# RWKV-7 chunk inverse on two chunks at a time, and norms per head spread by one product with ones

## The chip, the core and the metric

One NeuronCore of a Trainium2 chip runs the whole program. Its engines each work through their own instructions in order: TensorE (PE, with weight loads shown as PEld), VectorE (DVE), ScalarE (ACT), GpSimd (POOL), and SyncE (SP), which issues the DMAs. The metric is the device time of one execution in microseconds, the median of several runs.

## The reference

Two layers on 512 tokens of width 1024, in fp32. Each layer is half a SwiGLU feed-forward (1024 to 2816 and back), a mixer, and another half feed-forward, all with RMS norms. The mixer of layer 0 is RWKV-7 on 8 heads of 64 beside a block attention (MoBA) on 8 heads of 64. The mixer of layer 1 is HGRN2, a gated linear attention with 8 heads of 128. What the change touches:

```python
kk = _heads(k * k_k, RWKV_HEADS).astype(f32)
kk = kk * lax.rsqrt(jnp.maximum(jnp.sum(kk * kk, axis=-1, keepdims=True), 1e-24))
...
def step(state, inp):
    r_t, w_t, k_t, v_t, kk_t, a_t = inp
    sa = jnp.einsum('bhvk,bhk->bhv', state, -kk_t)
    state = (state * w_t[:, :, None, :]
             + jnp.einsum('bhv,bhk->bhvk', sa, kk_t * a_t)
             + jnp.einsum('bhv,bhk->bhvk', v_t, k_t))
    return state, jnp.einsum('bhvk,bhk->bhv', state, r_t)
...
y = ((y - mean) * lax.rsqrt(var + LNX_EPS)).reshape(bsz, seq, RWKV_DIM) * lnx_w + lnx_b
...
o = o * lax.rsqrt(jnp.mean(o * o, axis=-1, keepdims=True) + EPS)   # HGRN2, per head
```

## The kernel before

The tokens are split in two streams A and B of 256. Activations lie with the channel on the partitions. A long list of jobs, written out by hand in `build`, is the backbone: a job is one weight tile of 128 x 1024 (some 128 x 768), used in 24 (18) products of 256 columns into a PSUM bank `m`. Each weight is split in two planes for precision: `split_hi` copies the raw tile `wr` to `wh` on ScalarE, `split_lo` writes the rest to `wl` on VectorE, and `mm3` issues the three products hi x hi, hi x lo, lo x hi. Both planes have three buffers (`AHEAD + 1`). At the start of job n the program emits the split of job n + 2, behind the evictions of the job that has just ended.

Everything else runs as tasks: Python generators that emit a few instructions and yield. After every `mm3` a planner, `fill`, steps at most as many tasks as its own clock allows; the clock (`Clock`, `Eng`) keeps an assumed free time of each engine. These lines decide it:

```python
full = max(free["dve"], free["act"]) > now + self.left + BACK
for t in self.eligible():
    if t.ready <= max(now, free[t.eng]) + LEAD and (t.first or not full):
        self.step(t)
```

`left` is what remains of the current job by the planner's clock and `BACK` is 1 us. `need` forces a task to its end before the jobs behind it; it stands before the second stream's `proj0` blocks (`tail1`) and before the output projections.

The tasks that the change touches, per block q of 128 tokens (four in all), two chunks c of 64 tokens in each:

- `rw_front`: low-rank gates; the squares of k (`kk`); sums per head by four products with `sel` (two columns each) into a bank of 128 x 8; `rsqrt` on 128 x 8 (two integer operations, three Newton steps of three operations each); `bcast`, eight products of the broadcast result with the identity, which put the value of a head on all its partitions; then `kk` is scaled from PSUM.
- `rw_prep`, per chunk: the matrices `AR`, `BK`, `Ga`, `Gr`, then the start of the inverse (`X`, `Xt`).
- `rw_inv`, per chunk: five levels of a block inverse, each in two steps: eight products Ga x X into `zb`, a ScalarE copy to `Z`; eight products Z x Xt into `wt` and (but for the last level) eight Xt x Z into `wb`, written under a mask into `Xt` and `X` by VectorE.
- `rw_chain`, per chunk in order: the state.
- `rw_tail`: mean and variance per head; the same sums, `rsqrt` and `bcast` as in `rw_front`; gate; split to the planes of `y`.
- `hg_out` (HGRN2): output and state per four heads; sums of squares by eight products with `ones` (one column each); `rsqrt` on 128 x 8; for each four heads, four broadcast products with the identity, then scale, gate and split.

In the profile every instruction has the line of the wrapper in `Eng`, L176, so groups are told apart by their tiles: `b` is any of the five small PSUM banks of the tasks, `kms`, `rqi`, `rqy`, `rqz` are the tiles of the narrow `rsqrt`, and `cst` holds `ident`, `sel`, `blk` and `ones`. An fp32 product is two MATMUL instructions in the trace.

Of the kernel before, what the change touches and what calls it, by code (L numbers as in the profile page):

```python
# [26 lines left out]
EPS = 1e-6  # L27
# [163 lines left out]
class K:  # L191
# [85 lines left out]

    def rmask(self, i):
        return self.msk[:, i * 64:i * 64 + 64].unsqueeze(1).to_broadcast([128, 4, 64])

# [171 lines left out]
    def rsqrt(self, x, w, tag="rqy"):  # L452
        v = self.v
        i = self.t(self.hp, [128, w], I32, "rqi", 4)
        y = self.t(self.hp, [128, w], F32, tag, 4)
        z = self.t(self.hp, [128, w], F32, "rqz", 4)
        v.tensor_single_scalar(i, x.bitcast(I32), 1, op=ALU.logical_shift_right)
        v.tensor_scalar(y.bitcast(I32), i, -1.0, float(0x5f3759df), op0=ALU.mult, op1=ALU.add)
        for _ in range(3):
            v.tensor_tensor(z, x, y, op=ALU.mult)  # L460
            v.scalar_tensor_tensor(z, z, -0.5, y, op0=ALU.mult, op1=ALU.mult)
            v.scalar_tensor_tensor(y, z, 1.5, y, op0=ALU.add, op1=ALU.mult)
        return y
# [389 lines left out]
    def rwkv(self, st):  # L853
        h = st.i
        st.tails = []
        for q in (2 * h, 2 * h + 1):
            env = {}
            st.tails.append((q, env))
            c0, c1 = 2 * q, 2 * q + 1
            self.spawn(f"fe{q}", self.rw_front(st, q, env), ([f"prep{c0 - 1}"] if q else []) + ([f"tail{q - 2}"] if q > 1 else []))  # L860
            for c in (c0, c1):
                self.spawn(f"prep{c}", self.rw_prep(st, c, env),
                           [f"fe{q}"] + ([f"prep{c - 1}"] if c else []) + ([f"chain{c - 2}"] if c > 1 else []))
                self.spawn(f"inv{c}", self.rw_inv(env, c), [f"prep{c}"])
                self.spawn(f"chain{c}", self.rw_chain(env, c), [f"inv{c}"] + ([f"chain{c - 1}"] if c else []))

    def rw_front(self, st, q, env):
# [28 lines left out]
        for p in range(4):  # L896
            s.activation(at[:, p], za[:, p], AF.Tanh, scale=0.5, bias=der[:, 18 + p:19 + p])
        ss = self.bank(8)
        for p in range(4):
            mm(ss[:, 2 * p:2 * p + 2], sq[:, p], self.sel, start=True, stop=True)  # L900
        ms = self.t(pool, [128, 8], F32, "kms", 4)
        v.tensor_scalar(ms, ss, 1e-24, None, op0=ALU.max)
        rn = self.rsqrt(ms, 8)
        v.tensor_scalar(L, L, -0.5 * EXPM05, -0.5 * EXPM05, op0=ALU.mult, op1=ALU.add)
        for p in range(4):
            v.tensor_tensor_scan(L[:, p], self.c("reset"), L[:, p], 0.0, op0=ALU.mult, op1=ALU.add)
        yield
        bc = self.bank(4, 128)
        self.bcast(bc, rn)
        env["E1"] = E1 = self.t(pool, [128, 4, 2, 65], F32, "E1", 1)  # L910
        self.g.memset(E1[:, :, :, 0:1], 1.0)
        s.activation(E1[:, :, :, 1:65], L.rearrange("p a (c t) -> p a c t", c=2), AF.Exp)
        s.activation(L, L, AF.Exp, scale=-1.0)
        env["E2"] = L
        for p in range(4):
            v.scalar_tensor_tensor(kk[:, p], k[:, p], self.p("rw_k_k", p), bc[:, p], op0=ALU.mult, op1=ALU.mult)
        env["yq"] = km = q4("yq", 2)
# [7 lines left out]
        env["b"] = at  # L925

    def bcast(self, bc, rn):

        for p in range(4):
            for e in range(2):  # L930
                self.mm(bc[64 * e:64 * e + 64, p], rn[:, 2 * p + e:2 * p + e + 1].to_broadcast([128, 64]), self.ident,
                        start=True, stop=True)

    def rw_prep(self, st, c, env):
# [7 lines left out]
        def p4(tag, w=64, bufs=1):  # L942
            return self.t(pool, [128, 4, w], F32, tag, bufs)
# [33 lines left out]
        s.copy(BKt, tb)  # L977
        X, Xt = z["X"], z["Xt"] = p4("X", 64, 2), p4("Xt", 64, 2)
        idb = self.id64.unsqueeze(1).to_broadcast([128, 4, 64])
        s.copy(X, idb)  # L980
        s.copy(Xt, idb)
        yield
# [5 lines left out]
        s.copy(U0, ub)  # L988
        ab = self.bank(4, 64)
        for p in range(4):  # L990
            for e in range(2):
                h = slice(64 * e, 64 * e + 64)
                mm(ab[h, p], Ga[h, e, p], self.id64[h], start=True, stop=True)
        v.copy_predicated(X, self.rmask(0), ab)
        for e in range(2):
            h = slice(64 * e, 64 * e + 64)
            v.copy_predicated(Xt[h], self.rmask(len(RLEV))[h], Ga[h, e])

    def rw_inv(self, env, c):

        pool, v, s, mm = self.pool, self.v, self.s, self.mm
        z = env[c % 2]
        X, Xt, Ga = z["X"], z["Xt"], z["Ga"]
        he = [(p, e, slice(64 * e, 64 * e + 64)) for p in range(4) for e in range(2)]
        for lv in range(1, len(RLEV)):
            zb = self.bank(4, 64)
            for p, e, h in he:
                mm(zb[h, p], Ga[h, e, p], X[h, p], start=True, stop=True)
            Z = self.t(pool, [128, 4, 64], F32, "Z", 2)
            s.copy(Z, zb)  # L1010
            yield
            wt = self.bank(4, 64)
            for p, e, h in he:
                mm(wt[h, p], Z[h, p], Xt[h, p], start=True, stop=True)
            if lv < len(RLEV) - 1:
                wb = self.bank(4, 64)
                for p, e, h in he:
                    mm(wb[h, p], Xt[h, p], Z[h, p], start=True, stop=True)
                v.copy_predicated(X, self.rmask(lv), wb)
            v.copy_predicated(Xt, self.rmask(len(RLEV) + lv), wt)  # L1020
            yield

    def rw_chain(self, env, c):
# [8 lines left out]
        U = self.t(pool, [128, 4, 64], F32, "U", 1)  # L1032
        v.tensor_tensor(U, sb, z["U0"], op=ALU.add)
        yield
        sa = self.bank(4, 64)
# [6 lines left out]
        for p, e, h in he:  # L1042
            mm(sn[h, p], BKt[:, p, h], SV[e][:, p], start=True, stop=True)
        yb, yc = self.bank(4, 64), self.bank(4, 64)
        for p, e, h in he:
            mm(yb[h, p], SV[e][:, p], Gr[:, e, p], start=True, stop=True)
        for p, e, h in he:
            mm(yc[h, p], S0[h, p], AR[h, p, 1], start=True, stop=True)
        S1 = self.t(pool, [128, 4, 64], F32, "S0", 2)
        v.tensor_tensor(S1, sn, S0, op=ALU.add)  # L1050
        v.tensor_tensor(S1, S1, z["EL"].to_broadcast([128, 4, 64]), op=ALU.mult)
        self.S0 = S1
        ys = env["yq"][:, :, (c % 2) * 64:(c % 2) * 64 + 64]
        s.copy(ys, yb)
        v.tensor_tensor(ys, yc, ys, op=ALU.add)

    def rw_tail(self, st, q, env):
# [13 lines left out]
        yield  # L1071
        ss = self.bank(8)
        for p in range(4):
            mm(ss[:, 2 * p:2 * p + 2], sq[:, p], self.sel, start=True, stop=True)
        ms = self.t(pool, [128, 8], F32, "kms", 4)
        v.tensor_scalar(ms, ss, 1.0 / 64, LNX_EPS, op0=ALU.mult, op1=ALU.add)
        rn = self.rsqrt(ms, 8)
# [169 lines left out]
    def hg_out(self, st, q, env):  # L1247
# [30 lines left out]
        self.H0 = H1  # L1278
        ss = self.bank(8)
        for h in range(8):  # L1280
            mm(ss[:, h:h + 1], sq[:, h], self.ones, start=True, stop=True)
        ms = self.t(pool, [128, 8], F32, "kms", 4)
        v.tensor_scalar(ms, ss, 1.0 / 128, EPS, op0=ALU.mult, op1=ALU.add)
        rn = self.rsqrt(ms, 8)
        gt = sq
        v.tensor_scalar(gt, st.R["g"][:, :, sl], 0.5, 0.5, op0=ALU.mult, op1=ALU.add)
        yield
        for hb in range(2):
            bc = self.bank(4, 128)
            for j in range(4):  # L1290
                h = hb * 4 + j
                mm(bc[:, j], rn[:, h:h + 1].to_broadcast([128, 128]), self.ident, start=True, stop=True)
            for j in range(4):
                h = hb * 4 + j
                v.scalar_tensor_tensor(ot[:, h], ot[:, h], self.p("hg_norm_w", h), bc[:, j],
                                       op0=ALU.mult, op1=ALU.mult)
            hs = slice(hb * 4, hb * 4 + 4)
            v.tensor_tensor(ot[:, hs], ot[:, hs], gt[:, hs], op=ALU.mult)
            self.split(st.y[0][:, hs, sl], st.y[1][:, hs, sl], ot[:, hs])
            yield  # L1300
# [126 lines left out]
```

## Time and profile before

| | |
|---|---|
| median of 3 runs | 2280.84 us (2280.59 to 2281.16) |
| profiled execution | 2283.74 us |
| its span, first to last instruction | 2281.7 us |
| PE busy | 2247.5 us |
| PEld busy | 2177.4 us |
| DVE busy | 1640.6 us |
| ACT busy | 1061.6 us |
| mean granted TensorE clock | 0.996 |

Busy time of PE includes the modelled tails of pipelined matmuls. The starts of consecutive PE instructions give the better price of one. The profiled execution lasts 2 us longer than its span.

### The profile page before, as it was taken

What the parts mean: (1) busy time and instruction counts of PE and PEld (TensorE: products, weight loads), DVE (VectorE), ACT (ScalarE), POOL (GpSimd) and SP (SyncE); (2) the same over time, 40 slices, a digit from 0 to 9 for tenths busy, and PEclk for the clock granted to TensorE, in tenths of its full rate; (3) what the DMA queues carried; (4) which work ended last, traced back from release to release, by engine and by line L of the source; (5) the groups of instructions that cost most, each with busy time, mean ns of one, the idle gap of its engine ahead of it and who ended that gap; (6) DMA issues with size and microseconds to landing.
All of it is one profiled execution on the core that took longest, in us unless ns stands there. A gap on an engine that the chain in (4) does not pass through costs nothing.

```text
span 2281.7 us, 48851 instructions
## 1 busy us (share of the span) xinstructions
PE 2247.5 (99%) x20476; PEld 2177.4 (95%) x20476; DVE 1640.6 (72%) x2863; ACT 1061.6 (47%) x1716; POOL 4.8 (0%) x15
## 2 busy tenths in 40 slices
PE   8999999999999999999999999999999999999998
PEld 8999989899999898999998999999999999999998
DVE  6867758577677666776777786677777777667776
ACT  5545544345554434544454334454455334445444
POOL 0000000000000000000000000000000000000000
PEclk9999999999999999999999999999999999999999
DMA  6565524245554233445564344655665434556664
GB/s 224 183 194 172 168 89 141 88 138 175 188 174 150 75 109 96 148 159 183 181 187 159 130 139 150 191 178 179 193 188 172 149 120 147 164 190 187 189 195 134
DMA packets 107644, 363.64 MB, mean 159 GB/s; under 512 B 12064, under 2 KB 12192, under 8 KB 107296
## 3 DMA queue, kind: packets, MB, share of 16 engines
q1 hardware_dynamic: 107424, 360.53, 50.5%
q8 instruction: 160, 2.62, 0.5%
q14 instruction: 60, 0.49, 0.1%
HBM read 358.38 MB, written 2.10 MB: 158 GB/s over the span
## 4 chain that ended last, share of the span: by engine, by line
PE 91%; DVE 4%; ACT 2%; DMA 2%; issue 1%; SPq 0%; DVEq 0%; ACTq 0%
PE m L176 79%; PE b L176 12%; DVE wl L176 2%; ACT wh L176 1%; DMA wr<-in_f1gu 1%; DMA wr<-in_f2gu 1%; DVE x L176 0%; DVE tmp L176 0%; ACT hh L176 0%; DVE hl L176 0%; DVE m L176 0%; DVE acc L176 0%; DMA wr<-in_f1d 0%; DVE rqz L176 0%; ACT tmp L176 0%
## 5 line engine op out<-in xcount | busy, mean ns | idle before, releaser
L176 PE MATMUL m<-hh,wh 128*128 128x256 f32 x3808 | 1099.3, 289 | 14.2 <-ACT wh L176 11.4
L176 PE MATMUL m<-hh,wl 128*128 128x256 f32 x3808 | 1078.3, 283 | 6.6 <-DVE wl L176 6.6
L176 PE MATMUL m<-hl,wh 128*128 128x256 f32 x3808 | 1077.3, 283 | 0.5
L176 DVE TENSOR_TENSOR wl<-wr,wh 128x1024 fp32r<-128x1024 f32 (+2 forms) x725 | 831.9, 1151 | 316.1 <-ACT wh L176 307.3
L176 ACT CAST wh<-wr 128x1024 fp32r<-128x1024 f32 (+2 forms) x725 | 713.0, 990 | 546.8 <-PE m L176 386.9
L176 PEld LDWEIGHTS m<-hh,wh 128*128 128x128 f32 x3808 | 725.7, 191 | 29.2 <-ACT wh L176 12.2
L176 PEld LDWEIGHTS m<-hh,wl 128*128 128x128 f32 x3808 | 725.7, 191 | 9.7 <-DVE wl L176 9.7
L176 PEld LDWEIGHTS m<-hl,wh 128*128 128x128 f32 x3808 | 726.2, 191 | 2.6 <-DVE hl L176 1.6
L176 PE MATMUL m<-ah,wh 128*128 128x256 f32 x1408 | 398.6, 283 | 0.0
L176 PE MATMUL m<-al,wh 128*128 128x256 f32 x1408 | 390.0, 277 | 0.0
L176 PE MATMUL m<-ah,wl 128*128 128x256 f32 x1408 | 389.8, 277 | 0.0
L176 PEld LDWEIGHTS m<-ah,wh 128*128 128x128 f32 x1408 | 264.8, 188 | 7.6 <-issue 5.1
L176 PEld LDWEIGHTS m<-al,wh 128*128 128x128 f32 x1408 | 264.6, 188 | 1.0 <-issue 1.0
L176 PEld LDWEIGHTS m<-ah,wl 128*128 128x128 f32 x1408 | 264.6, 188 | 0.0
L176 ACT CAST ah<-tu 128x256 fp32r<-128x256 f32 x176 | 71.5, 406 | 309.1 <-DVE tu L176 309.1
L176 DVE SCALAR_TENSOR_TENSOR tu<-tu,m 128x256 f32<-128x256 f32 x352 | 146.9, 417 | 6.5 <-ACT tu L176 0.5
L176 DVE TENSOR_TENSOR al<-tu,ah 128x256 fp32r<-128x256 f32 x176 | 74.9, 425 | 84.3 <-ACT ah L176 84.3
L176 DVE SCALAR_TENSOR_TENSOR x<-m,x 128x512 f32<-128x512 f32 x128 | 87.9, 687 | 18.6 <-PE m L176 18.3
L176 DVE TENSOR_TENSOR m<-m,bc 128x512 f32<-128x512 f32 x118 | 82.0, 696 | 23.7 <-PE m L176 18.3
L176 ACT ACTIVATE tu<-m 128x256 f32<-128x256 f32 x176 | 66.7, 379 | 18.4 <-DVE m L176 18.1
L176 PE MATMUL b<-Rq,Rk 128*128 128x128 f32 (+2 forms) x576 | 59.5, 252 | 0.0
L176 PEld LDWEIGHTS b<-Rq,Rk 128*128 128x128 f32 (+2 forms) x576 | 55.3, 167 | 3.8
(204 smaller groups left out, 1456.8 us busy)
## 6 DMA issues: line engine op xcount, KB each, us to landing
wr<-in_f2gu SPq DMA_DIRECT2D x176, 512.0 KB, 3.5
wr<-in_f1gu SPq DMA_DIRECT2D x175, 512.0 KB, 3.5
wr<-in_f1d SPq DMA_DIRECT2D x96, 384.0 KB, 3.3
wr<-in_f2d SPq DMA_DIRECT2D x96, 384.0 KB, 3.2
wr<-in_od_in SPq DMA_DIRECT2D x48, 512.0 KB, 3.7
wr<-in_ev_in SPq DMA_DIRECT2D x44, 512.0 KB, 3.2
wr<-in_f1d SPq DMA_DIRECT2D x16, 512.0 KB, 3.6
wr<-in_ev_out SPq DMA_DIRECT2D x16, 512.0 KB, 3.7
```

Of the source, the lines that this page charges most:

```text
L176: return f(*args, **kw)
```

## The change

Two things are changed. The inverse of RWKV-7 becomes one task per block, `rw_inv(env)`, which starts after both chunks' `rw_prep`, holds both chunks in tiles of 128 x 8 x 64 and does both in every step; its start moves there from `rw_prep`. The sums of squares are taken by one product of 512 columns with a matrix of ones (`blk`, ones within a head of 64; a broadcast `ones` for heads of 128), which leaves the sum on every partition of the head; the narrow `rsqrt` and the broadcast products go, and `rsqrt_wide` does the same eleven operations on 128 x 512. Its two work tiles take the two buffers of `tmp`. One group of products and its copy moves to an earlier step in `rw_chain`.

```diff
+    def rsqrt_wide(self, x, n):
+        v = self.v
+        y, z = (self.t(self.hp, [128, n, 128], F32, "tmp", 2) for _ in range(2))
+        v.tensor_single_scalar(y.bitcast(I32), x.bitcast(I32), 1, op=ALU.logical_shift_right)
+        v.tensor_scalar(y.bitcast(I32), y.bitcast(I32), -1.0, float(0x5f3759df), op0=ALU.mult, op1=ALU.add)
+        for _ in range(3):
+            v.tensor_tensor(z, x, y, op=ALU.mult)
+            v.scalar_tensor_tensor(z, z, -0.5, y, op0=ALU.mult, op1=ALU.mult)
+            v.scalar_tensor_tensor(y, z, 1.5, y, op0=ALU.add, op1=ALU.mult)
+        return y
...
-                self.spawn(f"inv{c}", self.rw_inv(env, c), [f"prep{c}"])
-                self.spawn(f"chain{c}", self.rw_chain(env, c), [f"inv{c}"] + ([f"chain{c - 1}"] if c else []))
+            self.spawn(f"inv{q}", self.rw_inv(env), [f"prep{c1}"] + ([f"chain{c0 - 1}"] if q else []))
+            for c in (c0, c1):
+                self.spawn(f"chain{c}", self.rw_chain(env, c), [f"inv{q}"] + ([f"chain{c - 1}"] if c else []))
... (rw_front)
-        ss = self.bank(8)
-        for p in range(4):
-            mm(ss[:, 2 * p:2 * p + 2], sq[:, p], self.sel, start=True, stop=True)
-        ms = self.t(pool, [128, 8], F32, "kms", 4)
-        v.tensor_scalar(ms, ss, 1e-24, None, op0=ALU.max)
-        rn = self.rsqrt(ms, 8)
+        ss = self.bank(4, 128)
+        mm(ss, self.blk, sq, start=True, stop=True)
+        v.tensor_scalar(sq, ss, 1e-24, None, op0=ALU.max)
...
-        yield
-        bc = self.bank(4, 128)
-        self.bcast(bc, rn)
+        yield "dve"
...
+        rn = self.rsqrt_wide(sq, 4)
         for p in range(4):
-            v.scalar_tensor_tensor(kk[:, p], k[:, p], self.p("rw_k_k", p), bc[:, p], op0=ALU.mult, op1=ALU.mult)
+            v.scalar_tensor_tensor(kk[:, p], k[:, p], self.p("rw_k_k", p), rn[:, p], op0=ALU.mult, op1=ALU.mult)
... (rw_inv; X, Xt, ab and the masked copies into X and Xt move here from rw_prep)
+        X, Xt = (self.t(pool, [128, 8, 64], F32, n, 1) for n in ("X", "Xt"))
...
         for lv in range(1, len(RLEV)):
-            zb = self.bank(4, 64)
-            for p, e, h in he:
-                mm(zb[h, p], Ga[h, e, p], X[h, p], start=True, stop=True)
-            Z = self.t(pool, [128, 4, 64], F32, "Z", 2)
+            zb = self.bank(8, 64)
+            for i, p, j, e, h in he:
+                mm(zb[h, j], Ga[i][h, e, p], X[h, j], start=True, stop=True)
+            Z = self.t(pool, [128, 8, 64], F32, "Z", 1)
             s.copy(Z, zb)
... (wt and wb likewise; rw_chain: the products yc and s.copy(ys, yc) go into the first step, and the last adds yb)
... (rw_tail)
+        ss = self.bank(4, 128)
+        mm(ss, self.blk, sq, start=True, stop=True)
+        v.tensor_scalar(sq, ss, 1.0 / 64, LNX_EPS, op0=ALU.mult, op1=ALU.add)
         bb = self.bank(4, 128)
         mm(bb, self.blk, rk, start=True, stop=True)
         v.tensor_tensor(rk, bb, P["v"][:, :, sl], op=ALU.mult)
+        v.tensor_tensor(yq, self.rsqrt_wide(sq, 4), yq, op=ALU.mult)
         yield
-        bc = self.bank(4, 128)
-        self.bcast(bc, rn)
...
-        v.tensor_tensor(yq, bc, yq, op=ALU.mult)
... (hg_out)
         for hb in range(2):
-            bc = self.bank(4, 128)
+            hs = slice(hb * 4, hb * 4 + 4)
+            ss = self.bank(4, 128)
+            mm(ss, self.ones.to_broadcast([128, 128]), sq[:, hs], start=True, stop=True)
+            v.tensor_scalar(sq[:, hs], ss, 1.0 / 128, EPS, op0=ALU.mult, op1=ALU.add)
+        yield "dve"
...
+        for hb in range(2):
+            hs = slice(hb * 4, hb * 4 + 4)
+            rn = self.rsqrt_wide(sq[:, hs], 4)
             for j in range(4):
                 h = hb * 4 + j
-                mm(bc[:, j], rn[:, h:h + 1].to_broadcast([128, 128]), self.ident, start=True, stop=True)
...
```

## Rows read from the trace of the kernel before

**Rows 1.** The page, engines: busy us, share of the span, instructions.
```profile
PE 2247.5 (99%) x20476; PEld 2177.4 (95%) x20476; DVE 1640.6 (72%) x2863; ACT 1061.6 (47%) x1716; POOL 4.8 (0%) x15
```
**Rows 2.** The page, chain that ended last, share of the span by line.
```profile
PE m L176 79%; PE b L176 12%; DVE wl L176 2%; ACT wh L176 1%; DMA wr<-in_f1gu 1%; DMA wr<-in_f2gu 1%; DVE x L176 0%; DVE tmp L176 0%; ACT hh L176 0%; DVE hl L176 0%; DVE m L176 0%; DVE acc L176 0%; DMA wr<-in_f1d 0%; DVE rqz L176 0%; ACT tmp L176 0%
```
**Rows 3.** Waits of PE for `wl`: us in total, times, longest us.
```profile
PE m L176 <- DVE wl L176: 6.6, 11, 0.8
```
**Rows 4.** Groups of PE by shape: busy us, mean ns of one.
```profile
L176 PE MATMUL b<-cst,rqy 128*64 128x128 f32 x128 | 8.7, 279 | 0.0
...
L176 PE MATMUL b<-cst,rqy 128*128 128x128 f32 x64 | 8.4, 274 | 0.0
...
L176 PE MATMUL b<-cst,sq 128*128 128x1 f32 x64 | 7.4, 245 | 0.0
...
L176 PE MATMUL b<-yq,cst 128*128 128x512 f32 x8 | 4.2, 605 | 0.3 <-DVE yq L176 0.3
L176 PE MATMUL b<-cst,Pr 128*128 128x2 f32 x32 | 3.8, 241 | 0.0
```
**Rows 5.** Timeline of PE, one inverse step among weight products: start, us.
```profile
403.97 0.28 PE L176 MATMUL m<-hh,wl 128*128 128x256 f32 x1
404.18 0.68 PE L176 MATMUL b<-X,Ga 64*64 64x64 f32 x16
...
405.02 0.28 PE L176 MATMUL m<-hl,wh 128*128 128x256 f32 x1
405.13 0.28 PE L176 MATMUL m<-hh,wl 128*128 128x256 f32 x1
```
**Rows 6.** Timeline of PE, two groups of an inverse step back to back.
```profile
394.37 0.68 PE L176 MATMUL b<-Xt,Z 64*64 64x64 f32 x16
394.88 0.63 PE L176 MATMUL b<-Z,Xt 64*64 64x64 f32 x16
```
**Rows 7.** Groups of DVE by shape.
```profile
L176 DVE TENSOR_TENSOR yq<-yq,Pk 128x512 f32<-128x512 f32 x4 | 2.8, 694 | 0.1
...
L176 DVE TENSOR_SCALAR rqy<-rqi 128x8 int32<-128x8 int32 x12 | 2.1, 172 | 0.4
...
L176 DVE TENSOR_SCALAR L<-L 128x512 f32<-128x512 f32 x4 | 1.7, 420 | 0.0
```
**Rows 8.** Timeline of DVE, last step of `tail1` between two splits of weights.
```profile
480.05 2.36 DVE L176 TENSOR_TENSOR wl<-wr,wh 128x1024 fp32r<-128x1024 f32 x2 [0.53 <-PE m L176]
...
483.05 1.11 DVE L176 TENSOR_SCALAR yq<-yq,par 128x128 f32<-128x128 f32 x4
...
486.99 0.87 DVE L176 SCALAR_TENSOR_TENSOR tu<-tu,m 128x256 f32<-128x256 f32 x2
...
489.28 2.36 DVE L176 TENSOR_TENSOR wl<-wr,wh 128x1024 fp32r<-128x1024 f32 x2 [0.52 <-ACT wh L176]
```
**Rows 9.** Timeline of PE, the first use of the weights split at 489.28.
```profile
490.87 0.28 PE L176 MATMUL m<-hh,wl 128*128 128x256 f32 x1
```
**Rows 10.** Stretches: length, PE, PEld, DVE, ACT, POOL busy, clock, DMA share, GB/s.
```profile
372.54:381.93 9.39, 9.39 (x104) 8.41 (x104) 7.63 (x25) 2.46 (x7) 0.00 (x0) 1.00 0.14 48
174.02:177.43 3.41, 3.41 (x16) 3.41 (x17) 2.77 (x5) 1.38 (x3) 0.00 (x0) 0.50 0.64 186
1237.00:1437.00 200.00, 199.65 (x1671) 193.93 (x1671) 149.43 (x278) 81.09 (x120) 0.00 (x0) 1.00 0.45 142
```
**Rows 11.** Timeline of ACT in `hg_out` of block 1.
```profile
1412.93 0.62 ACT L176 CAST hh<-ot 128x512 fp32r<-128x512 f32 x1 [3.37 <-DVE ot L176]
1413.46 1.78 ACT L176 CAST wh<-wr 128x768 fp32r<-128x768 f32 x2
```
**Rows 12.** Timeline of PE, its waits just ahead of 174.02.
```profile
172.68 0.39 PE L176 MATMUL m<-hh,wh 128*128 128x256 f32 x1 [1.62 <-ACT wh L176]
...
173.94 0.54 PE L176 MATMUL m<-hh,wl 128*128 128x256 f32 x1 [0.76 <-DVE wl L176]
```
**Rows 13.** Tile Plr on DVE: ns min/median/max, first and last start.
```profile
L176 DVE SCALAR_TENSOR_TENSOR Plr<-m,der,sh x2: 477/477/477, 221.8 to 600.3; 128x256 f32<-128x256 f32 x2
```

More of the change, by code (lines that the diff above doesn't have):

```diff
@@ L276, in p, with rmask @@
         return self.par[:, o:o + n]
-    def rmask(self, i):
-        return self.msk[:, i * 64:i * 64 + 64].unsqueeze(1).to_broadcast([128, 4, 64])
+    def rmask(self, i, n=4):
+        return self.msk[:, i * 64:i * 64 + 64].unsqueeze(1).to_broadcast([128, n, 64])
     def hmask(self, i):
@@ L925, in rw_front @@
         env["b"] = at
[L927 to L932, printed above, removed]
     def rw_prep(self, st, c, env):
@@ L977, in rw_prep @@
         s.copy(BKt, tb)
[L978 to L981, printed above, removed]
         yield
@@ L988, in rw_prep, with rw_inv @@
         s.copy(U0, ub)
-        ab = self.bank(4, 64)
-        for p in range(4):
+    def rw_inv(self, env):
+        pool, v, s, mm = self.pool, self.v, self.s, self.mm
+        Ga = [env[i]["Ga"] for i in range(2)]
+        X, Xt = (self.t(pool, [128, 8, 64], F32, n, 1) for n in ("X", "Xt"))
+        for i in range(2):
+            env[i]["Xt"] = Xt[:, 4 * i:4 * i + 4]
+        idb = self.id64.unsqueeze(1).to_broadcast([128, 8, 64])
+        s.copy(X, idb)
+        s.copy(Xt, idb)
+        he = [(i, p, 4 * i + p, e, slice(64 * e, 64 * e + 64)) for i in range(2) for p in range(4) for e in range(2)]
+        ab = self.bank(8, 64)
+        for i, p, j, e, h in he:
+            mm(ab[h, j], Ga[i][h, e, p], self.id64[h], start=True, stop=True)
+        v.copy_predicated(X, self.rmask(0, 8), ab)
+        for i in range(2):
@@ L991, in rw_prep @@
             for e in range(2):
                 h = slice(64 * e, 64 * e + 64)
[L993 to L1004, printed above, removed]
+                v.copy_predicated(Xt[h, 4 * i:4 * i + 4], self.rmask(len(RLEV))[h], Ga[i][h, e])
@@ L1005, in rw_inv @@
+        yield
         for lv in range(1, len(RLEV)):
-            zb = self.bank(4, 64)
-            for p, e, h in he:
-                mm(zb[h, p], Ga[h, e, p], X[h, p], start=True, stop=True)
-            Z = self.t(pool, [128, 4, 64], F32, "Z", 2)
+            zb = self.bank(8, 64)
+            for i, p, j, e, h in he:
+                mm(zb[h, j], Ga[i][h, e, p], X[h, j], start=True, stop=True)
+            Z = self.t(pool, [128, 8, 64], F32, "Z", 1)
             s.copy(Z, zb)
             yield
-            wt = self.bank(4, 64)
@@ L1013, in rw_inv @@
-            for p, e, h in he:
-                mm(wt[h, p], Z[h, p], Xt[h, p], start=True, stop=True)
+            wt = self.bank(8, 64)
+            for i, p, j, e, h in he:
+                mm(wt[h, j], Z[h, j], Xt[h, j], start=True, stop=True)
             if lv < len(RLEV) - 1:
[L1016 to L1020, printed above, removed]
+                wb = self.bank(8, 64)
+                for i, p, j, e, h in he:
+                    mm(wb[h, j], Xt[h, j], Z[h, j], start=True, stop=True)
+                v.copy_predicated(X, self.rmask(lv, 8), wb)
@@ L1021, in rw_inv @@
+            v.copy_predicated(Xt, self.rmask(len(RLEV) + lv, 8), wt)
             yield
@@ L1033, in rw_chain @@
         v.tensor_tensor(U, sb, z["U0"], op=ALU.add)
+        yc = self.bank(4, 64)
+        for p, e, h in he:
+            mm(yc[h, p], S0[h, p], AR[h, p, 1], start=True, stop=True)
+        ys = env["yq"][:, :, (c % 2) * 64:(c % 2) * 64 + 64]
+        s.copy(ys, yc)
         yield
@@ L1043, in rw_chain @@
             mm(sn[h, p], BKt[:, p, h], SV[e][:, p], start=True, stop=True)
-        yb, yc = self.bank(4, 64), self.bank(4, 64)
+        yb = self.bank(4, 64)
         for p, e, h in he:
             mm(yb[h, p], SV[e][:, p], Gr[:, e, p], start=True, stop=True)
-        for p, e, h in he:
-            mm(yc[h, p], S0[h, p], AR[h, p, 1], start=True, stop=True)
         S1 = self.t(pool, [128, 4, 64], F32, "S0", 2)
@@ L1052, in rw_chain @@
         self.S0 = S1
-        ys = env["yq"][:, :, (c % 2) * 64:(c % 2) * 64 + 64]
-        s.copy(ys, yb)
-        v.tensor_tensor(ys, yc, ys, op=ALU.add)
+        v.tensor_tensor(ys, yb, ys, op=ALU.add)
     def rw_tail(self, st, q, env):
@@ L1071, in rw_tail @@
         yield
[L1072 to L1077, printed above, removed]
+        ss = self.bank(4, 128)
+        mm(ss, self.blk, sq, start=True, stop=True)
+        v.tensor_scalar(sq, ss, 1.0 / 64, LNX_EPS, op0=ALU.mult, op1=ALU.add)
         bb = self.bank(4, 128)
@@ L1278, in hg_out @@
         self.H0 = H1
[L1279 to L1287, printed above, removed]
-        for hb in range(2):
-            bc = self.bank(4, 128)
+        for hb in range(2):
+            hs = slice(hb * 4, hb * 4 + 4)
[3 more added lines that the diff above has]
+        yield "dve"
+        gt = st.R["g"][:, :, sl]
+        v.tensor_scalar(gt, gt, 0.5, 0.5, op0=ALU.mult, op1=ALU.add)
+        for hb in range(2):
+            hs = slice(hb * 4, hb * 4 + 4)
+            rn = self.rsqrt_wide(sq[:, hs], 4)
             for j in range(4):
                 h = hb * 4 + j
-                mm(bc[:, j], rn[:, h:h + 1].to_broadcast([128, 128]), self.ident, start=True, stop=True)
-            for j in range(4):
-                h = hb * 4 + j
-                v.scalar_tensor_tensor(ot[:, h], ot[:, h], self.p("hg_norm_w", h), bc[:, j],
+                v.scalar_tensor_tensor(ot[:, h], ot[:, h], self.p("hg_norm_w", h), rn[:, j],
                                        op0=ALU.mult, op1=ALU.mult)
-            hs = slice(hb * 4, hb * 4 + 4)
             v.tensor_tensor(ot[:, hs], ot[:, hs], gt[:, hs], op=ALU.mult)
```

## Prediction

> **What bounds the kernel now.** I read the page first. TensorE is busy over 99% of the span and VectorE over 72% [rows 1]. The chain that ended last lies on TensorE: 79% of the span in the weight products, 12% in the small products of the tasks [rows 2]. So a microsecond taken from TensorE's own stream is a microsecond of time, as long as the weights keep coming. Next the waits: over the whole program TensorE waits for `wl`, the plane that VectorE writes, only 6.6 us, never more than 0.8 us at once [rows 3]. The reader is to see two things in this: the change's gain on TensorE is real, and VectorE has so far never been late by much. Everything then hangs on how late VectorE can be, and that is read from the timeline around the longest pieces of other work between two splits of weights.
>
> **TensorE: the sums of squares.** I price products by busy time of their groups [rows 4]. Removed: the broadcast products of `rw_front` and `rw_tail` (8.7 us), those of `hg_out` (8.4), its one-column sums (7.4), and the two-column sums of `rw_tail` (3.8) and of `rw_front`, of the same form and number (3.8 again). That is 32.1 us. Added: 4 products of 512 columns in `rw_front`, 4 in `rw_tail`, 8 in `hg_out`. The trace has four such products with `blk`, 8 instructions in 4.2 us, so 1.05 us each and 16.8 us for 16. TensorE gains 15.3 us.
>
> **TensorE: the inverse.** The products are the same in number; only the gaps between weight products in which they lie become fewer. A lone group of 16 instructions stretches the distance between its neighbours from 403.97 to 405.02, so 1.05 us for the group and two plain products; the next plain one follows 0.11 us later, so the group costs 0.81 to 0.83 [rows 5]. A second group that starts in the same gap follows 0.51 us behind the first [rows 6]. Entering and leaving the gap thus costs 0.30 us. Five levels of two steps for four blocks are 40 gaps saved: 12 us. Moving the first step out of `rw_prep` makes 12 gaps of 8: 1.2 us back. `rw_chain` has three groups and one group in two gaps, afterwards two and two: nothing. Gain 10.8 us; it is between 0, if two chunks' steps shared their gaps already, and 12. I take 10.8, since the rows shown are separate gaps. The inverse's evictions on VectorE and ScalarE get fewer and longer; I count them at nothing, as they lie beside weight products. Its longer chain (both chunks wait for the slower) costs nothing either: `tail1` is through before the split at 489.28 [rows 8], and the first job that needs it out of the way writes `Plr` at 600.3 [rows 13]. That is 110 us of cover; without it each step more would cost its whole latency.
>
> Together TensorE's stream gets 26 us shorter.
>
> **VectorE: the price.** `rsqrt_wide` is nine operations with two tensor inputs on 128 x 512, at 0.694 each, and two integer ones. The trace has integer ones on narrow tiles only (0.172); on 128 x 512 an fp32 TENSOR_SCALAR takes 0.42 [rows 7]. The integer pair lies between 0.42 and 0.694 each; I take 0.42, the row of the same operation: 9 x 0.694 + 2 x 0.42 = 7.1 us, at most 7.6. The narrow one takes 11 x 0.172 = 1.9.
>
> The Trainium skill (VectorE: DVE Perf Modes, What auto-detection actually checks) makes the rate depend on a single source and on both ends lying in SBUF with even dimensions, not on the type. By that rule the integer pair runs at 0.42 and the call at 7.1 us; at the rate of the two-input row it would be 7.6, or 9 us more VectorE time over 16 calls. No row of the kernel before has the wide integer form.
>
> There are 16 calls (four in `rw_front`, four in `rw_tail`, eight in `hg_out`), and 16 evictions of a full bank at 0.69 for 12 narrow ones: 16 x 7.1 - 12 x 1.9 + 16 x 0.69 - 12 x 0.17 = +100 us. VectorE goes from 1641 to some 1740 us, 76% of the span. On average there is room, in the HGRN2 stretch less: it is busy 149 of 200 us there now [rows 10] and gets 27 more for two blocks (four calls and their evictions less two narrow calls).
>
> **What is late next.** What matters is that each call stands in one step, emitted at once, and the next job's `wl` is emitted behind it. Work in one piece: `rw_front` 7.1 + 1.1 + 1.1 (four operations on 128 columns each, 1.11 [rows 8]) + 0.7 = 10.0 us; `rw_tail` 0.7 + 0.7 + 7.1 + 0.7 = 9.2; each half of `hg_out` 7.1 + 1.1 + 0.7 = 8.9 until `ot` stands, then ScalarE's copy of 0.62 [rows 11] and another 0.7.
>
> How much can TensorE bear? In the last step of `tail1` the splits end at 482.41 and the next starts at 489.28 [rows 8]; the first of its two planes takes half of 2.36 us and is ready at some 490.5, and TensorE wants it at 490.87 [rows 9]. So 6.87 + 0.4 = some 7.2 us between splits is all that it bears where it has weight products alone. Into that time also go the feed-forward's own evictions, 0.87 us of `tu` at the least [rows 8]. A step of 9.2 to 10.2 us with 0.9 beside it is late by 2.9 to 3.9 us; I take 4, since more than one eviction falls due in 10 us. The other end: from 372.54 to 381.93 there was no split for 9.4 us, and TensorE did not idle, because 104 instructions lay there [rows 10] where weight products alone, at the 0.11 us of [rows 5], would be 85; wider ones of the tasks filled the rest. There a step is covered, late by 0.
>
> For the eight calls of `rw_front` and `rw_tail` I take the middle, 2 us: I assume that half of them stand among dense task products, as the one at 372 does. For the eight of `hg_out` I take 4, since only the levels of the next block lie beside, and 1 more for ScalarE: its copy `hh<-ot` waits for the scaled `ot`, and two casts to `wh` follow it with no gap [rows 11], so the first plane of the weights is held up too. 8 x 2 + 8 x 5 = 56 us. The bounds are 0 and 8 x 4 + 8 x 6 = 80.
>
> **The sum.** -26 + 56 = +30 us. The profiled execution has a span of 2281.7 us and a time 2 us longer, 2283.7; its forecast is 2314. The median of the runs is 2280.8, so 2311.
>
> **Rivals.**
> 1. VectorE's work is covered, and the kernel is faster. The mechanism is `fill`: it steps a task only while VectorE's planned backlog ends within 1 us of the job's end, so a long step starts on an idle engine, and task products stretch the jobs that follow, as at 372. For it: VectorE idles 28% [rows 1], and 9.4 us without a split passed. Against it: the test sees the backlog before the step, not its length, and while VectorE is behind, the same test keeps back the task products that would be the cover. It decides where a call makes weights late by less than 26 / 16 = 1.6 us. With full cover: 2280.8 - 26 = 2255.
> 2. The stalls feed themselves. After waits of 1.62 and 0.76 us [rows 12] the granted clock in 174.02 to 177.43 is 0.50, the 1.2 GHz level, and 16 products take 3.41 us [rows 10], 1.6 us more than at 0.11. With that behind each of 16 stalls and the upper bound of lateness: -26 + 80 + 26 = +80, 2361. Against it: at the lower clock VectorE catches up, so part is given back. The two `tmp` buffers that a call holds belong here: ScalarE's squares of the norms wait for them.
> The Trainium skill (TensorE: Matmul & The Clock Gate, HAM oscillation) has gaps in the matmul stream bring the clock down again, at each of them. By that rule every stall of 4 us pays this; the one stretch shown agrees.
> 3. The two-chunk inverse doesn't save its gaps, because the planner already put steps of both chunks side by side: 2311 + 11 = 2322.
> 4. Small lateness just eats the gain: 2276 to 2290.
>
> **How the numbers follow.** The forecast, with rival 3 in it, 2290 to 2332: 0.50. Rival 1, 2254 to 2276: 0.27. Rival 2, over 2332: 0.15. Rival 4: 0.08. Below 2260 lies about a third of rival 1, above 2342 about two thirds of rival 2, so 2260 to 2342 holds 8 in 10; the forecast's own range is 2290 to 2332. 0.2%, 4.6 us, is about what a measurement of this kernel can tell from no change. Slower by more: the forecast, rival 2 and a part of rival 4, 0.67. Within it: 0.06. Faster: 0.27.
>
> **What would show it.** The wide calls: VectorE busy near 1740 us, the operations at 0.69. The gain: the groups `b<-cst,rqy` and `b<-cst,sq` gone, 16 products of 512 columns, inverse groups in gaps of 32 and 64. The loss: `PE m <- DVE wl` from 6.6 us to some 40, with single waits of 3 to 5 us, and `<- ACT wh` in `hg_out`; a lower clock behind them. If those waits stay under 20 us, rival 1 is right and my reading of one step at 482 to 489 as the limit is what failed.

## The result, and the profile after

The changed kernel takes 2381.54 us (median of 4 runs, 2376.51 to 2382.77) against 2280.72 us before (4 runs): ratio 1.0437, 95% interval 1.0421 to 1.0454. It is 101 us slower; 2311 us was forecast, the range 2290 to 2332, and 2260 to 2342 as the bounds that hold 8 in 10. The profiled execution took 2382.57 us with a span of 2380.5 us; its mean granted TensorE clock is 0.972, before 0.996.

The page, engines and chain by line, of the changed kernel (for [rows 1, 2]):

```profile
PE 2258.8 (95%) x20188; PEld 2185.3 (92%) x20188; DVE 1736.1 (73%) x2871; ACT 1057.7 (44%) x1688; POOL 4.8 (0%) x15
...
PE m L176 71%; PE b L176 11%; DVE tmp L176 5%; DVE wl L176 3%; ACT wh L176 2%; DVE ot L176 1%; DMA wr<-in_f2gu 0%; DVE x L176 0%; DVE tu L176 0%; ACT hh L176 0%; DVE m L176 0%; DVE hl L176 0%; DMA wr<-in_f1gu 0%; DVE acc L176 0%; DVE kk L176 0%
```

VectorE's busy time is what was forecast, some 1740 us. But `DVE tmp`, the work tiles of the wide call, is now 5% of the chain that sets the end, from 0%: nothing lies over these operations any more.

Groups of PE and of VectorE by shape (for [rows 4, 7]): busy us, mean ns of one.

```profile
L176 PE MATMUL b<-X,Ga 64*64 64x64 f32 x640 | 23.1, 222 | 0.0
L176 PE MATMUL b<-Xt,Z 64*64 64x64 f32 x640 | 23.0, 222 | 0.0
L176 PE MATMUL b<-Z,Xt 64*64 64x64 f32 x512 | 17.6, 218 | 0.0
...
L176 PE MATMUL b<-sq,cst 128*128 128x512 f32 x16 | 7.5, 592 | 0.0
...
L176 PE MATMUL b<-kk,cst 128*128 128x512 f32 x8 | 4.5, 645 | 0.0
...
L176 PE MATMUL b<-Pr,cst 128*128 128x512 f32 x8 | 4.1, 592 | 0.0
```
```profile
L176 DVE SCALAR_TENSOR_TENSOR tmp<-tmp,tmp 128x512 f32<-128x512 f32 x96 | 66.5, 692 | 3.3
...
L176 DVE TENSOR_SCALAR tmp<-tmp 128x512 int32<-128x512 int32 x16 | 6.8, 427 | 0.5
```

The 16 products with ones take 7.5 + 4.5 + 4.1 = 16.1 us. The operations of a call take the 0.69 and 0.42 us that were forecast. So the work was priced rightly. The waits of PE were not (for [rows 3]): us in total, times, longest.

```profile
PE m L176 <- ACT wh L176: 69.7, 14, 8.2
PE m L176 <- DVE wl L176: 38.4, 28, 6.6
```

Together 108.1 us. Before it was 18.0: 6.6 for `wl` [rows 3], and for `wh`

```profile
PE m L176 <- ACT wh L176: 11.4, 5, 6.2
```

There are sixteen new stalls of TensorE, of 1.8 to 8.2 us, one behind each wide call. This is VectorE around the first (for [rows 8]), start and duration in us:

```profile
260.92 1.23 DVE L176 TENSOR_TENSOR wl<-wr,wh 128x1024 fp32r<-128x1024 f32 x1 [0.71 <-ACT wh L176]
262.06 0.42 DVE L176 TENSOR_SCALAR tmp<-kk 128x512 int32<-128x512 int32 x1
262.52 0.43 DVE L176 TENSOR_SCALAR tmp<-tmp 128x512 int32<-128x512 int32 x1
262.98 0.69 DVE L176 TENSOR_TENSOR tmp<-kk,tmp 128x512 f32<-128x512 f32 x1
263.71 1.42 DVE L176 SCALAR_TENSOR_TENSOR tmp<-tmp,tmp 128x512 f32<-128x512 f32 x2
...
269.52 1.14 DVE L176 SCALAR_TENSOR_TENSOR kk<-Pk,par,tmp 128x128 f32<-128x128 f32 x4
270.57 1.11 DVE L176 TENSOR_SCALAR yq<-at,der 128x128 f32<-128x128 f32 x4
271.72 0.69 DVE L176 SCALAR_TENSOR_TENSOR Pk<-yq,Pk 128x512 f32<-128x512 f32 x1
272.33 1.22 DVE L176 TENSOR_TENSOR wl<-wr,wh 128x1024 fp32r<-128x1024 f32 x1
```

The eleven operations run from 262.06 to 269.5, 0.73 us apart, and the step until 272.33: 10.2 us between two splits, the 10.0 of the prediction. TensorE at that place:

```profile
268.39 0.28 PE L176 MATMUL m<-hl,wh 128*128 128x256 f32 x1
273.60 0.58 PE L176 MATMUL m<-hh,wl 128*128 128x256 f32 x1 [4.93 <-DVE wl L176]
```

And the stretches around two stalls (columns as in [rows 10]):

```profile
262.06:268.40 6.34, 6.34 (x56) 6.34 (x54) 6.03 (x11) 3.21 (x5) 0.00 (x0) 1.00 0.26 84
...
707.20:715.28 8.08, 0.00 (x0) 0.00 (x0) 6.85 (x18) 1.40 (x3) 0.00 (x0) 0.78 0.00 0
715.28:721.90 6.62, 6.16 (x27) 5.86 (x28) 4.75 (x6) 2.96 (x5) 0.00 (x0) 0.50 0.47 158
```

TensorE ran 56 instructions under the call at 262, all of them weight products, and then had no weights. Between the splits around the sixteen calls there are no task products at all in eleven cases, 1 to 10 instructions in the other five.

The worst stall goes through ScalarE (for [rows 11]); its queue in the feed-forward and in `hg_out`, and the product that waits for the first:

```profile
702.37 0.64 ACT L176 ACTIVATE L<-L 128x512 f32<-128x512 f32 x1
713.88 0.41 ACT L176 CAST ah<-tu 128x256 fp32r<-128x256 f32 x1 [10.88 <-DVE tu L176]
714.19 1.99 ACT L176 CAST wh<-wr 128x1024 fp32r<-128x1024 f32 x2
...
1368.43 0.62 ACT L176 CAST hh<-ot 128x512 fp32r<-128x512 f32 x1 [15.34 <-DVE ot L176]
1368.96 1.04 ACT L176 CAST wh<-wr 128x1024 fp32r<-128x1024 f32 x1
```
```profile
715.28 0.58 PE L176 MATMUL m<-hh,wh 128*128 128x256 f32 x1 [8.16 <-ACT wh L176]
```

The copy `ah<-tu` is the feed-forward's own; it waits for `tu`, which stands behind the call in VectorE's queue, and the two casts to `wh` stand behind the copy. So the call holds up both planes of the weights, the one that VectorE doesn't write too.

**Where the 99 us of span went.** I summed the distances from the start of each PE instruction to the next over the trace, by tile. The small products take 255.3 us instead of 277.8: -22.5. The weight products take 2112.3 instead of 1991.0: +121.4. Of these 108.1 - 18.0 = 90 are the waits. The other 31 are what is left over, and fit the products at the lower clock: the mean of 0.972 means some (1 - 0.972) x 2380.5 / 0.5 = 133 us at the 1.2 GHz level, before 18 us; in 715.28 to 721.90 above, 27 products take 6.62 us, 0.245 each with their waits, instead of the 0.113 in 262.06 to 268.40. A count in the trace comes to the same: 330 weight products that are followed by another without a wait lie at the lower level, 0.225 us from start to start against 0.122 at the higher, which makes 34 us; before there were 43 of them, 4 us.

### The profile page after: what moved, and what is told of

Read it like the earlier page. It is cut to its first block, busy times and chain, and to the rows that moved or that the text cites. A ratio compares the mean times of both kernels' runs of the same rounds, so it can differ in the third digit from the quotient of the medians.

```text
span 2380.5 us, 48195 instructions
## 1 busy us (share of the span) xinstructions
PE 2258.8 (95%) x20188; PEld 2185.3 (92%) x20188; DVE 1736.1 (73%) x2871; ACT 1057.7 (44%) x1688; POOL 4.8 (0%) x15
## 4 chain that ended last, share of the span: by engine, by line
PE 81%; DVE 13%; ACT 3%; issue 2%; DMA 1%; SPq 0%; DVEq 0%; ACTq 0%
PE m L176 71%; PE b L176 11%; DVE tmp L176 5%; DVE wl L176 3%; ACT wh L176 2%; DVE ot L176 1%; DMA wr<-in_f2gu 0%; DVE x L176 0%; DVE tu L176 0%; ACT hh L176 0%; DVE m L176 0%; DVE hl L176 0%; DMA wr<-in_f1gu 0%; DVE acc L176 0%; DVE kk L176 0%
## 5 line engine op out<-in xcount | busy, mean ns | idle before, releaser
L176 PE MATMUL m<-hh,wh 128*128 128x256 f32 x3808 | 1111.0, 292 | 41.3 <-ACT wh L176 40.2
L176 PE MATMUL m<-hh,wl 128*128 128x256 f32 x3808 | 1089.7, 286 | 26.7 <-DVE wl L176 26.7
L176 PEld LDWEIGHTS m<-hh,wh 128*128 128x128 f32 x3808 | 735.8, 193 | 58.8 <-ACT wh L176 41.8
L176 PEld LDWEIGHTS m<-hh,wl 128*128 128x128 f32 x3808 | 735.0, 193 | 31.9 <-DVE wl L176 31.9
L176 PEld LDWEIGHTS m<-hl,wh 128*128 128x128 f32 x3808 | 735.8, 193 | 4.4 <-issue 3.1
L176 PE MATMUL m<-ah,wl 128*128 128x256 f32 x1408 | 398.7, 283 | 11.7 <-DVE wl L176 11.7
L176 PE MATMUL m<-al,wh 128*128 128x256 f32 x1408 | 397.6, 282 | 0.1
L176 PEld LDWEIGHTS m<-ah,wh 128*128 128x128 f32 x1408 | 272.3, 193 | 34.6 <-ACT wh L176 30.5
L176 DVE TENSOR_TENSOR al<-tu,ah 128x256 fp32r<-128x256 f32 x176 | 74.9, 426 | 84.3 <-ACT ah L176 84.3
L176 DVE SCALAR_TENSOR_TENSOR x<-m,x 128x512 f32<-128x512 f32 x128 | 87.9, 687 | 20.5 <-PE m L176 20.3
L176 DVE TENSOR_TENSOR m<-m,bc 128x512 f32<-128x512 f32 x118 | 82.0, 696 | 19.6 <-PE m L176 16.1
L176 DVE SCALAR_TENSOR_TENSOR tmp<-tmp,tmp 128x512 f32<-128x512 f32 x96 | 66.5, 692 | 3.3
```

Of the source, the lines that this page charges most:

```text
L176: return f(*args, **kw)
```

## The experiments

**The length of the call.** The wide call of the changed kernel with one and with six Newton steps instead of three, so work is left out in one and superfluous in the other:

```diff
-        for _ in range(3):
+        for _ in range(1):      # e5; range(6) in e6
```

> The changed kernel with one Newton step instead of three in the wide inverse square root (two of three are left out of the computation): six operations of 0.69 us fewer, a call of 3.1 us instead of 7.3. Theory (a call in one piece makes the next weights late by its length beyond what TensorE can bear; with 5.6 us of lateness on a call of 7.3, and every call late): a call 4.2 us shorter is late by 1.4 us, 16 x 1.4 = 23 us of waits instead of 90, little of it at the lower clock; time 2381 - 67 - some 25 of clock = 2280 to 2300, waits for wl and wh together 25 to 45 us. Rival (VectorE as a whole has too little room): 67 us less VectorE work is 3% of its span, and the time would fall by that much at most in proportion to its 73% share, to some 2330 or more. Rival (the wide products or the two-chunk inverse cost the time, not the calls): stays at 2381.

> The changed kernel with six Newton steps instead of three in the wide inverse square root (more work than the reference needs): nine operations more per call, a call of 13.6 us instead of 7.3. Theory: nothing covers the additional time, so each of the 16 calls adds its 6.3 us to the wait behind it: waits 90 + 100 = 190 us, time 2381 + 100 and up to 15 of lower clock = 2475 to 2500. Rival (a call is covered by task products that the planner puts beside it, and only the first part of a call is paid): time under 2440. Rival (the time is lost elsewhere): 2381.

Measured: 2302.83 us with one step (2 runs), 2488.99 with six (2 runs). The page (engines) and the waits of PE, one step:

```profile
PE 2237.0 (97%) x20188; PEld 2163.1 (94%) x20188; DVE 1669.0 (73%) x2775; ACT 1059.0 (46%) x1688; POOL 4.7 (0%) x15
```
```profile
PE m L176 <- ACT wh L176: 25.1, 13, 5.7
PE m L176 <- DVE wl L176: 19.7, 30, 2.3
```

and six steps:

```profile
PE 2261.6 (91%) x20188; PEld 2186.9 (88%) x20188; DVE 1836.5 (74%) x3015; ACT 1058.2 (43%) x1688; POOL 3.7 (0%) x15
```
```profile
PE m L176 <- ACT wh L176: 133.6, 14, 14.9
PE m L176 <- DVE wl L176: 76.1, 25, 13.2
```

| Newton steps | VectorE per call, against three | waits, `wh` + `wl` | waits per call, against three | median |
|---|---|---|---|---|
| 1 | -67.1 / 16 = -4.2 us | 44.8 us | -4.0 us | 2302.8 us |
| 3 | | 108.1 us | | 2381.5 us |
| 6 | +100.4 / 16 = +6.3 us | 209.7 us | +6.4 us | 2489.0 us |

Each microsecond of a call is a microsecond of waiting, down to a call of some 3 us, where 1.8 us per call are still left over the 16.5 of the two-chunk inverse with narrow norms (below). From three to six steps every one of the sixteen stalls grew, by 5.5 to 6.8 us, where a call grew by 6.5 from its first operation to its last: nowhere was there cover for the additional length. With one step, behind four calls no stall of more than 0.5 us is left. With six steps VectorE is busy for no more than 74% of the span: the average says nothing of it. With one step the time is a few microseconds above what was expected.

**The calls in pieces.** First only the tiles: the result of a call goes into a tile that is dead at that place and the scratch into a PSUM bank, so that `tmp` stays free. Then the same with a step boundary after every Newton step:

```diff
-    def rsqrt_wide(self, x, n):
+    def rsqrt_wide(self, x, y, z=None):
...
         for _ in range(3):
+            z = self.bank(4, 128)
             v.tensor_tensor(z, x, y, op=ALU.mult)
             v.scalar_tensor_tensor(z, z, -0.5, y, op0=ALU.mult, op1=ALU.mult)
             v.scalar_tensor_tensor(y, z, 1.5, y, op0=ALU.add, op1=ALU.mult)
+            yield "dve"         # e4 alone
```

> The change, but the wide rsqrt keeps its result in a tile that is dead at that place and its scratch in a small PSUM bank, so that no call holds a tmp buffer; same operations, still in one piece. If the length of the piece on VectorE makes the loss, nothing changes: 2375 to 2388 us, and the 16 waits stay. If ScalarE's wait for the two tmp buffers makes it: under 2340 us.

> As e3, but the task gives way (yield) after every Newton step of the wide rsqrt, so that the splits of weights can go in between; the same operations and the same VectorE time, in pieces of at most 3 us. If the length of one piece makes the loss, most of the 16 waits go: 2258 to 2280 us, PE waits under 30 us, clock back to 0.99. If it is VectorE's sum of work (1736 us busy), nothing is gained: 2370 us or more.

Measured: with its own tiles 2385.03 us (1 run), far from the 2340 of the other case: the two buffers of `tmp` are not the cause. Cut, 2290.0 us (6 runs, 2289.03 to 2293.11), ratio to before 1.0032, interval 1.002 to 1.0044. VectorE and the waits of PE, calls cut:

```profile
265.90 0.70 DVE L176 SCALAR_TENSOR_TENSOR b<-b,yq 128x512 f32<-128x512 f32 x1
266.63 0.69 DVE L176 SCALAR_TENSOR_TENSOR yq<-b,yq 128x512 f32<-128x512 f32 x1
267.24 1.22 DVE L176 TENSOR_TENSOR wl<-wr,wh 128x1024 fp32r<-128x1024 f32 x1
268.37 0.69 DVE L176 TENSOR_TENSOR b<-kk,yq 128x512 f32<-128x512 f32 x1
```
```profile
PE m L176 <- ACT wh L176: 13.3, 7, 6.0
PE m L176 <- DVE wl L176: 11.6, 24, 1.0
PE m L176 <- ACT hh L176: 9.2, 4, 6.6
PE b L176 <- DVE acc L176: 6.9, 2, 5.8
```

The split at 267.24 now stands between two Newton steps. VectorE does the same operations, and 91 of the 101 us are gone. So what cost the time is that a call is one piece, not VectorE's total. The time is still 10 us above the range that was expected; the last group of experiments looks at that.

**The two parts alone.** The kernel before with the two-chunk inverse alone (with its part of `rw_chain`), and the changed kernel with the inverse of before, which leaves the wide norms alone:

```diff
-                self.spawn(f"inv{c}", self.rw_inv(env, c), [f"prep{c}"])
+            self.spawn(f"inv{q}", self.rw_inv(env), [f"prep{c1}"] + ([f"chain{c0 - 1}"] if q else []))
```

> The kernel before with the two-chunk inverse alone; norms as before. If the loss comes from the wide calls on VectorE, this kernel has only the gain on TensorE: 2280.7 - 11 = 2270 us (2265 to 2278), waits of PE for wl and wh together no more than 25 us. If the loss comes from the longer chain of the inverse (both chunks must be ready, and nothing else to do), it is slower than before, 2330 us or more.

> The change with the inverse of the kernel before; only the sums of squares and the wide rsqrt. If the wide calls make the loss: 2381.5 + 11 = 2392 us (2378 to 2400), 16 waits of PE of 2 to 9 us. If the inverse makes it: under 2300 us.

Measured: the inverse alone 2268.07 us (4 runs), ratio 0.9941, interval 0.9924 to 0.9958; once more, beside the last two kernels below, 2270.72 us (4 runs), 0.9953, interval 0.9936 to 0.9971. It gains 11 to 15 us. The norms alone 2393.51 us (4 runs), ratio 1.0483, interval 1.0467 to 1.0498: they cost 111 us. -15 and +111 make +96, within 5 us of the whole.

**By place.** The two-chunk inverse with the wide norms in HGRN2 alone, in one piece:

> The changed kernel with the narrow norms of the kernel before in RWKV-7's two places; HGRN2's keep the wide form (8 of 16 calls), and the two-chunk inverse stays. The trace of the changed kernel shows 51 us of waits behind HGRN2's eight calls and 40 us behind the other eight. Theory: TensorE -13 (inverse) - 10 (HGRN2's sums of squares), +51 of waits, +15 of lower clock: 2281 + 43 = 2315 to 2335. Rival (the loss sits in the feed-forward stretches, where the planner has no other products, and HGRN2's are covered): 2265 to 2290. Rival (HGRN2 alone carries the loss): 2360 or more.

Measured: 2336.75 us (4 runs), ratio 1.0242, interval 1.0227 to 1.0258; some 66 us over the inverse alone, a little more than expected, so HGRN2's eight calls carry over half of the loss. The waits of PE for `wh` there are 58.3 us. In the changed kernel's list of stalls, eight in `hg_out` of 4.9 to 6.4 us make 47, or 51 with the short waits for `wl` behind them, and the other eight, of 1.8 to 8.2 us, make 39.

**The Newton steps on GpSimd.** VectorE keeps the two integer operations; twelve operations of a call go to GpSimd, with a step boundary behind:

```diff
+        v = self.g
         for _ in range(3):
             v.tensor_tensor(z, x, y, op=ALU.mult)
-            v.scalar_tensor_tensor(z, z, -0.5, y, op0=ALU.mult, op1=ALU.mult)
-            v.scalar_tensor_tensor(y, z, 1.5, y, op0=ALU.add, op1=ALU.mult)
+            v.tensor_tensor(z, z, y, op=ALU.mult)
+            v.tensor_scalar(z, z, -0.5, 1.5, op0=ALU.mult, op1=ALU.add)
+            v.tensor_tensor(y, z, y, op=ALU.mult)
...
+        yield "dve"
```

> The changed kernel with the result of a call in dead tiles and the Newton steps of the wide call on GpSimd (four operations a step there, twelve a call, the two integer operations stay on VectorE), and a step boundary behind the call, so that VectorE writes the next weight plane while GpSimd works. Theory (VectorE's piece in front of the next weight plane is the cause): waits of TensorE for wl and wh back to 15 to 30 us, time 2255 to 2285, below the kernel before. Rival 1 (GpSimd and VectorE hinder each other, or GpSimd is slow by a factor of two or more, so that a call lasts 20 us or more and the norm tasks themselves become late): VectorE's own operations get longer than 0.69 us and the time is 2290 to 2340. Rival 2 (something else than VectorE's queue makes the weights late): stays near 2381.

Measured: 2332.06 us (4 runs), ratio 1.0214, interval 1.0197 to 1.0231. Rival 1 of the expectation holds in the time and in VectorE's longer operations (last section); the call shown here lasts 16.2 us, from 1366.75 to 1382.99, not 20. GpSimd and VectorE in `hg_out` of block 1:

```profile
1372.16 1.33 POOL L176 TENSOR_TENSOR Rq<-Rk,Rq 128x512 f32<-128x512 f32 x1
```
```profile
1371.52 0.83 DVE L176 TENSOR_TENSOR Rq<-Rq,tt 128x256 f32<-128x256 f32 x1
1372.27 1.24 DVE L176 TENSOR_TENSOR tt<-tt 128x8 f32<-128x8 f32 x1
1383.02 1.14 DVE L176 SCALAR_TENSOR_TENSOR ot<-ot,par,Rq 128x128 f32<-128x128 f32 x4 [9.52 <-POOL Rq L176]
```

VectorE's next operation, `ot`, is in its queue already while GpSimd still works on `Rq`. It waits 9.5 us, and the splits of the weights behind it wait too; TensorE waits 9.5 us for `wh` at 1386.54. Here the piece has changed its owner, not its place in the queue. But only two of the sixteen calls show such a wait of VectorE for GpSimd, 19.1 us together. How the rest of the loss divides, beyond the longer operations, was not taken apart.

**Pieces in one place each.** The two-chunk inverse and the cut calls in HGRN2 alone, in RWKV-7 alone, and in neither:

> Two-chunk inverse, narrow norms in RWKV-7's two places, wide norms in HGRN2 with the call cut after every Newton step (8 calls). Theory (a call costs because it is one piece; cut, it costs little, and its product with ones saves some 10 us of TensorE): waits under 35 us, time 2255 to 2280. Rival (HGRN2's blocks have too little room on VectorE even for pieces, the 30 us that the fully cut kernel lacks to its floor lie here): 2280 to 2295.

> Two-chunk inverse, narrow norms in HGRN2, wide norms in RWKV-7's two places with the call cut after every Newton step (8 calls). Theory (as for HGRN2 alone, with some 5 us of TensorE saved): waits under 35 us, time 2260 to 2280. Rival (the 30 us that the fully cut kernel lacks lie here): 2280 to 2295.

> The two-chunk inverse with the narrow norms of the kernel before everywhere, again, beside the two kernels with cut calls. Expected as in its first run: 2266 to 2273. It is the best version if neither of the two others is below it.

Measured side by side: HGRN2 cut 2284.98 us (10 runs, ratio 1.0012, interval 1.0002 to 1.0021), RWKV-7 cut 2276.58 us (10 runs, 0.9977, 0.9967 to 0.9987), neither 2270.72. The best version is the inverse alone, though its interval, 0.9936 to 0.9971, just touches that of RWKV-7 cut. The theory of the second expectation holds (2260 to 2280), that of the first doesn't; its rival is right, weakly: HGRN2's part costs 14 us over the inverse alone, RWKV-7's 6, and 20 together is what separates the kernel with all calls cut from the inverse alone. One place of it is seen in the kernel with HGRN2 cut, ahead of the output projection, where `need` forces the last task to its end:

```profile
2012.61 1.22 DVE L176 TENSOR_TENSOR wl<-wr,wh 128x1024 fp32r<-128x1024 f32 x1
2013.74 0.69 DVE L176 TENSOR_TENSOR b<-sq,Rq 128x512 f32<-128x512 f32 x1
...
2018.12 1.14 DVE L176 SCALAR_TENSOR_TENSOR ot<-ot,par,Rq 128x128 f32<-128x128 f32 x4
...
2021.61 1.23 DVE L176 TENSOR_TENSOR wl<-wr,wh 128x1024 fp32r<-128x1024 f32 x1 [0.25 <-ACT wh L176]
```

Two Newton steps and the scaling stand together again, 7.9 us between splits, and the product behind waits 6.6 us for `hh`. What the rest of the 14 us is stays open. RWKV-7's 6 us have a place too: with RWKV-7 cut TensorE waits once 5.5 us for `acc`, the squares summed for an RMS norm, at 1150 us, and with all calls cut 5.8 us at 1149; with HGRN2 cut the waits for `acc` come to 0.3 us, and with the inverse alone there are none. Why that wait arises there stays open.

## Why the prediction was wrong

The sign and the mechanism were right: the call stands in one piece in front of the next split, the weights come late behind it, and cutting the piece takes the loss away. Rival 1 was wrong: beside eleven of the sixteen calls the planner put no product of a task. What failed is the lateness, taken as 56 us where 90 were measured, and the clock, which was left out of the sum.

- **TensorE, -26 us.** The inverse's three groups take 63.7 us of busy time instead of 74.9 (27.3, 27.3 and 20.3); alone it gives 11 to 15 us, forecast 10.8, and its longer chain cost no wait (16.5 us in all for `wh` and `wl`). The products with ones take 16.1 us for 16.8. By the distances of starts both parts give 22.5. Right within 4 us. (One reading was off: the two-column sums of `rw_front` had a group of their own before, `b<-cst,kk`, of 4.2 us, not 3.8.)
- **VectorE's price, 7.1 us a call, +100 us.** 1736.1 us busy, +96; a call lasts 7.4 from its first operation to its last. Right. The integer pair runs at 0.42 to 0.43, as the rule of the Trainium skill (VectorE: DVE Perf Modes, What auto-detection actually checks) had it.
- **Lateness in `rw_front` and `rw_tail`, "the middle, 2 us".** This step failed. It rested on the assumption that "half of them stand among dense task products, as the one at 372 does". All eight were late, 39 us in all, 4.9 each: +23. Of this 16 is the assumption itself, eight calls late by 4 us in place of four. The other 7 lies in what TensorE bears: between the splits around these calls stand 9.7 to 13.1 us, 11.1 in the mean, about what was forecast; less the stalls, TensorE bore 6.2 us in the mean, not the 7.2 read at one place in `tail1`. The row of 372.54 to 381.93 [rows 10] was misread. This is TensorE of the kernel before inside that stretch:

```profile
375.78 1.09 PE L176 MATMUL b<-cst,rqy 128*64 128x128 f32 x16
376.80 1.16 PE L176 MATMUL b<-Pg,g 128*128 128x128 f32 x8
```

The first of these groups is `bcast`, which the change takes away. And the stretch was several short steps, each of which had brought its own products for TensorE. A wide call is 7.4 us in one step and brings no product of its own. How much of the cover each of the two took away isn't shown.

- **Lateness in `hg_out`, 5 us.** 51 / 8 = 6.4: +11. Here the term was mis-sized. For the calls of `rw_front` and `rw_tail` ScalarE was left out of the price altogether: the feed-forward's copy `ah` waits behind the call as `hh` does in `hg_out`, and holds the casts to `wh`; two of those eight stalls, of 8.2 and 4.0 us, end with `wh`.
- **The clock, 0 us in the forecast.** 31 us as what is left over, 30 by the count of products. This term failed too. It was priced in rival 2 (+26) and left out of the sum, against the one pair of rows that showed it [rows 10, 12]. The Trainium skill (TensorE: Matmul & The Clock Gate, HAM oscillation) says that gaps in the matmul stream bring the clock down again; the 0.50 right behind the 8.16 us wait agrees. Not every wait did it: fifteen of the sixteen stalls have a stretch at the lower level in or behind them, but behind the shortest, of 1.82 us, the clock stays at 1.00 (418.31 to 425.14). "The stalls feed themselves" had been given 0.15, and came about.

The sum as measured: -22.5 + 39 + 51 + 31 = +98.5, against 98.8 by the spans. It must come out so, since the 31 are what was left over; with the 30 that were counted it is +97.5. Rival 2's 2361 has nearly the right clock cost, 26, and the wrong bound: its upper bound of 80 us for the lateness was still below the 90 measured, since it allowed for 4 us at a call of `rw_front` or `rw_tail`, where stalls reached 8.2.

## What to carry to other kernels

Work on an engine that also feeds the bound one costs by its longest uninterrupted piece between two feeds, not by its sum: read the distance between feeds in the trace before, and look at what else is on the bound engine at that very place after the change, since cover may consist of the work that the change removes. Follow the feed through every in-order queue that it passes, for a copy that waits on the long piece holds up the other plane too. And where the trace of before shows the clock fall behind waits of a microsecond or two, put it into the sum for the stalls that are forecast; here fifteen of sixteen paid it.

## What was not expected of the hardware

While a GpSimd operation with two inputs ran, VectorE operations with two inputs took longer, even the shortest: `tt<-tt` on 128 x 8, 0.16 us when GpSimd is idle (at 1366.68), took 1.24, from 1372.27 to 1373.51; the GpSimd operation above ran from 1372.16 to 1373.49. It ends when the other ends. The Trainium skill (SBUF — State Buffer, SBUF: two separate sides) says that such a pair excludes each other for a whole instruction, and these rows agree. Single split operations of 1024 columns, 1.23 us otherwise, took 2.01 us in the same stretch:

```profile
1366.68 0.16 DVE L176 TENSOR_TENSOR tt<-tt 128x8 f32<-128x8 f32 x1
...
1368.15 2.01 DVE L176 TENSOR_TENSOR wl<-wr,wh 128x1024 fp32r<-128x1024 f32 x1
```

So the GpSimd version also pays on the weights: VectorE was busy 1713.6 us there, where the 144 operations that left it (100 us at 0.69) should have taken it to some 1636.

The cost of the lower clock hardly grew with the length of the stalls. With six Newton steps the mean granted clock is 0.954, some 229 us at the lower level instead of 133; but the waits are 102 us longer than with three and the time 107, so that nearly all of the additional time at the lower level lies inside the stalls, where it costs nothing. The records of the clock agree: TensorE stood still during 134 us of the lower level with six steps, during 42 with three.
